# Seven block products for eight in the up projections of three feed-forward nets of a decoder trunk, on one Trainium2 core

## The chip, the core and the metric

The kernel runs on one core of a Trainium2 chip. The metric is the time on the device in microseconds (us), as the median of several runs. Before the change three runs gave 2679.24, 2676.48 and 2678.54 us, so the median is **2678.54 us**.

The engines are named as the profile names them: PE is the tensor engine (matmuls), PEld its weight loads, DVE the vector engine, ACT the scalar engine, POOL is GpSimd, SP is the engine that issues most transfers (DMA).

## What is computed

One step of a decoder trunk with two layers, for 544 tokens in all: 512 of a prompt and 32 of samples (8 sequences of 4 tokens). The model width is 1024. Each layer is a feed-forward net (ffn1), a mixing half (attention beside a convolution) and a second feed-forward net (ffn2), with a layer norm behind each:

```
def swiglu(x, w_up, w_down):                    # w_up 1024 x 5632, w_down 2816 x 1024
    a, u = jnp.split(x @ w_up, 2, axis=-1)
    return (jax.nn.silu(a) * u) @ w_down

x = layer_norm(ALPHA * x + 0.5 * swiglu(x, p['ffn1_up'], p['ffn1_down']), p['ln1_g'], p['ln1_b'])
q, k, v, glu, gates = jnp.split(x @ p['w_in'] + p['b_in'], SPLITS, axis=-1)
...
x = layer_norm(ALPHA * x + mix @ p['w_out'], p['ln2_g'], p['ln2_b'])
x = layer_norm(ALPHA * x + 0.5 * swiglu(x, p['ffn2_up'], p['ffn2_down']), p['ln3_g'], p['ln3_b'])
```

All tensors are float32. There are four feed-forward nets in the program: ffn1 and ffn2 of layer 0, ffn1 and ffn2 of layer 1, in this order, each pair with a mixing half between.

## The kernel before

Features lie on the 128 partitions, tokens on the free axis. The activations X are four tiles (`pr` in the profile), each with two chunks of 128 features x 544 tokens. The tokens are worked in two parts, cut at 280: `hf` 0 has 280 columns, `hf` 1 has 264.

**Halves of a number.** PE works on the type fp32r. To keep float32 accuracy each operand is held as two tiles, a high one (a cast on ACT: L251 for weights, L301 for activations) and the rest (a subtraction on DVE: L254, L302). A product takes three matmuls: `wh` by h, `wh` by lo, `wl` by h (L292 to L294, in `unit`). A unit is 256 output columns (two of 128, `m`) for one token part: with 8 chunks `k` of the inner dimension it has 8 x 2 x 3 = 48 matmuls, into one PSUM tile `pa`.

**A feed-forward net** (`ffn`, L410) has 11 column blocks j of 256 columns, in groups of 3, 3, 3 and 2. For a block, `up` (L432) makes two units of the gate weights (key "a"), each followed by a SiLU on ACT (L418), then two units of the other weights ("u"), each followed by the product on DVE (L424) and a split into halves (L301, L302). `up_first` (L441) does blocks 0 and 1, all of token part 0 ahead of part 1, because the norm before it delivers X in two parts. After the first block of a group, the down products of the group before are made (`down`, L458) and added into the residual tiles Y on DVE (L456). Block 10 and the last group end the net, with the layer norm (`tail`, `ln_fin`). `residual` (L400) makes the start of Y, ALPHA times X, from the two halves of X: a multiplication on ACT and L405 on DVE.

**Weights.** `plan` lists all pieces of weights in the order of use. `fetch` loads the next piece (256 columns x 8 chunks, 1 MB) by a DMA on SP (L162) into a tile `raw` of a pool of its own (`wp`, three buffers of 8 KB per partition). `prep` splits it by two casts of 1024 elements per partition on ACT and two subtractions on DVE into `wh` and `wl`, which are tiles of the large pool `pp` (36 buffers of 4 KB, called "pair", shared with X, Y, H and the tiles of attention). `W` hands out the next piece, and first calls `prep` until LA pieces (2; LAU 3 and LAV 2 in the up projections) are under way. Pool `fp` (6 buffers, tiles `f`) holds small activations. PSUM has three tiles of two banks (`ps2`, named `pa`) and two of one bank (`ps1`, named `pb`).

**What sets the order.** The program is written once in Python; a scheduler of the tile framework then puts each engine's instructions in one order, and each engine runs them strictly in that order. An instruction waits for the tiles that it reads, and for the buffer that it writes to be released.

**The mixing half** (`mix`, L716) makes keys, values, queries, gates and a gated input of a convolution by units of the same kind; the first weights are "k" and "ug", whose unit is followed by sigmoids on ACT (L771). The taps of the convolution (L806) run on DVE.

Of the kernel before, what the change touches and what calls it, by code (L numbers as in the profile page):

```python
# [25 lines left out]
CUT = 280  # L26
# [27 lines left out]
LA, LAU, LAV, TAP, LAG, WPB, FPB = 2, 3, 2, 1.2, 0.0, 3, 6  # L54
# [6 lines left out]
TF = 0  # L61
PPB = 36
# [34 lines left out]
class Ker:  # L97
    def __init__(self, ctx, tc, a):
# [3 lines left out]
        self.wp = pool("wp", WPB)  # L102
# [52 lines left out]
    def plan(self):  # L155
# [74 lines left out]
    def fetch(self, cut=0):  # L230
        """the load of the next piece of weights, in cut parts"""
        key, kk, load = self.pieces[self.loaded]
        self.loaded += 1
        raw = self.wp.tile([128, 8, 256], F32, tag="raw", name=self.nm("raw"))
        n = kk // max(cut, 1)
        for k in range(0, kk, n):
            dma = load(raw[:, k:k + n], k) if cut > 1 else load(raw[:, :kk])
            if cut:
                self.tc.keep_in_program_order(dma)
        return key, kk, raw  # L240

    def prep(self, pin=False, got=None):
        nc = self.nc
        key, kk, raw = got or self.fetch()
        ms = []
        for k in range(0, kk, 4):
            n = min(4, kk - k)
            src = raw[:, k:k + n, :]
            wh = self.pp.tile([128, 4, 256], F32R, tag="pair", name=self.nm("wh"))
            wl = self.pp.tile([128, 4, 256], F32R, tag="pair", name=self.nm("wl"))  # L250
            ins = nc.scalar.copy(wh[:, :n], src)  # L251
            if pin:
                self.tc.keep_in_program_order(ins)
            ins = nc.vector.tensor_tensor(wl[:, :n], src, wh[:, :n].bitcast(F32), op=ALU.subtract)  # L254
# [10 lines left out]
    def ahead(self, n):  # L265
        """n pieces of weights, and no more, split before what follows"""
# [44 lines left out]
    def ln_fin(self, acc, Y, hf, emit):  # L311
        """the norm from the sums on, in two steps, each begun by products"""
# [49 lines left out]
    def rsqrt(self, src, n, w):  # L362
        """1 / sqrt(src + EPS) for a few columns: a seed from the bits, one step of Newton's, one of third order"""
# [20 lines left out]
    def ln_out(self, X, l, vg, vb, func=AF.Identity):  # L384
        vec = self.vec[l]

        def emit(p, y, hs):
            xf = self.f1([128, 2, hs.stop - hs.start])
            for m in range(2):
                c = 2 * p + m  # L390
                self.nc.scalar.activation(xf[:, m], y[:, m, hs], func,  # L391
                                          scale=vec[:, vg + c:vg + c + 1], bias=vec[:, vb + c:vb + c + 1])
            xh, xl = X[p]
            self.split(xh[:, :, hs], xl[:, :, hs], xf)
        return emit

# [832 lines left out]
```

## Time and profile before

| what | value |
|---|---|
| median of three runs | 2678.54 us |
| span of the profiled execution | 2676.0 us (the page gives no other time of this execution) |
| POOL busy | 282.4 us, 11% |
| L292, L293, L294 (the split products) | 6336 matmuls each, of 20638 on PE |
| largest idle times of PE by what ended them, by the groups of its lines | 11.5 us DVE L254, 6.7 us and 4.8 us DVE L302 |
| transfers | 232.14 MB, mean 87 GB/s |

The busy time of an engine is the time in which an instruction of it was under way; the share is of the span. Matmuls overlap, so the mean duration of one (about 0.29 us) is more than twice the distance between two (0.125 us). The lines of the page and of the trace on which the argument rests are shown where it is made.

### The profile page before, as it was taken

The page shows a single profiled execution, that of the slowest core. Times are in us where ns is not written, and L with a number is a line of the kernel's source. Part 1 is how long each engine was busy: PE and PEld are TensorE (multiplying, and loading weights), DVE is VectorE, ACT ScalarE, POOL GpSimd, SP SyncE. Part 2 cuts the span into 40 slices and gives each one's busy share as a digit, 9 for nine tenths or more (in the row PEclk, how much of TensorE's full clock was granted, in tenths as well). Part 3 has the DMA queues.
Part 4 walks back from the last instruction along what each step waited for, and adds up shares of the span by engine and source line. Part 5 has one row for each costly group of instructions (what it writes and reads, how often), then busy time and mean ns, then how long its engine had stood idle before and what let it go on. Part 6 is the DMA issues. An engine that isn't in the chain of part 4 may idle for free.

```text
span 2676.0 us, 47289 instructions
## 1 busy us (share of the span) xinstructions
PE 2610.9 (98%) x20638; PEld 2561.6 (96%) x20638; DVE 1430.8 (53%) x2135; ACT 978.6 (37%) x1646; POOL 282.4 (11%) x532
## 2 busy tenths in 40 slices
PE   8999999999999999999999999999999999999997
PEld 7999999989899999999999999999899999999997
DVE  4323246897976554243453233469989665433235
ACT  4222125577426342222242222246863352422211
POOL 2000001532300000000110000025141000000001
PEclk9999999999999999999999999999999999999998
DMA  7223133222322233132332222233223222222221
GB/s 222 82 83 107 48 111 83 59 86 66 83 86 80 73 99 107 64 102 73 110 111 95 79 91 76 72 83 87 69 63 103 79 94 80 80 91 86 80 84 42
DMA packets 250089, 232.14 MB, mean 87 GB/s; under 512 B 40433, under 2 KB 247485, under 8 KB 249785
## 3 DMA queue, kind: packets, MB, share of 16 engines
q1 hardware_dynamic: 246073, 220.35, 26.7%
q0 software_dynamic: 3808, 8.76, 1.1%
q8 instruction: 162, 2.65, 0.4%
q14 instruction: 46, 0.38, 0.0%
HBM read 225.69 MB, written 9.16 MB: 88 GB/s over the span
## 4 chain that ended last, share of the span: by engine, by line
PE 86%; DVE 5%; POOL 3%; ACT 2%; issue 1%; DMA 1%; SPq 0%; DVEq 0%; POOLq 0%; ACTq 0%
PE pa L292 27%; PE pa L294 27%; PE pa L293 27%; DVE pr L806 2%; POOL f L821 2%; DVE wl L254 1%; PE pa L916 1%; PE pb L945 1%; PE pb L957 1%; DMA raw<-in_ffn_up_dram 1%; DVE pr L302 1%; POOL nw L372 0%; PE pb L353 0%; ACT wh L251 0%; PE pa L1039 0%
## 5 line engine op out<-in xcount | busy, mean ns | idle before, releaser
L292 PE MATMUL pa<-pr,wh 128*128 128x264 f32 (+2 forms) x6336 | 1838.7, 291 | 19.2 <-DVE pr L302 4.8
L293 PE MATMUL pa<-pr,wh 128*128 128x264 f32 (+2 forms) x6336 | 1831.8, 289 | 6.7 <-DVE pr L302 6.7
L294 PE MATMUL pa<-pr,wl 128*128 128x264 f32 (+2 forms) x6336 | 1825.7, 289 | 11.5 <-DVE wl L254 11.5
L292 PEld LDWEIGHTS pa<-pr,wh 128*128 128x128 f32 x6336 | 1193.2, 189 | 27.5 <-ACT pr L301 5.8
L294 PEld LDWEIGHTS pa<-pr,wl 128*128 128x128 f32 x6336 | 1196.2, 189 | 13.7 <-DVE wl L254 12.8
L293 PEld LDWEIGHTS pa<-pr,wh 128*128 128x128 f32 x6336 | 1195.9, 189 | 10.8 <-DVE pr L302 8.8
L254 DVE TENSOR_TENSOR wl<-raw,wh 128x1024 fp32r<-128x1024 f32 (+1 forms) x424 | 483.0, 1165 | 191.0 <-ACT wh L251 190.5
L251 ACT CAST wh<-raw 128x1024 fp32r<-128x1024 f32 (+1 forms) x424 | 406.3, 999 | 403.7 <-PE pa L293 324.5
L424 DVE TENSOR_TENSOR f<-pa,f 128x560 f32<-128x560 f32 (+2 forms) x88 | 63.6, 722 | 536.2 <-PE pa L294 496.9
L806 DVE SCALAR_TENSOR_TENSOR pr<-u,cw,pr 128x512 f32<-128x512 f32 x480 | 344.9, 768 | 1.7 <-ACT pr L799 1.7
L301 ACT CAST pr<-f 128x560 fp32r<-128x560 f32 (+1 forms) x162 | 102.4, 646 | 356.7 <-DVE f L424 302.1
L418 ACT ACTIVATE f<-pa 128x560 f32<-128x560 f32 (+2 forms) x88 | 54.9, 624 | 428.4 <-PE pa L294 428.1
L371 POOL TENSOR_SCALAR nw<-nw 94x3 f32<-94x3 f32 (+3 forms) x16 | 7.0, 436 | 1712.1 <-DVE nw L367 1712.1
L456 DVE SCALAR_TENSOR_TENSOR pr<-pa,pr 128x560 f32<-128x560 f32 (+3 forms) x128 | 92.3, 722 | 165.8 <-PE pa L294 165.4
L302 DVE TENSOR_TENSOR pr<-f,pr 128x560 fp32r<-128x560 f32 (+1 forms) x162 | 115.6, 723 | 55.0 <-ACT pr L301 53.8
L821 POOL TENSOR_TENSOR f<-f,cw 128x124 f32<-128x124 f32 x128 | 103.6, 847 | 1.6 <-ACT f L760 1.4
L391 ACT ACTIVATE f<-pr,vec 128x280 f32<-128x280 f32 (+1 forms) x80 | 42.6, 604 | 82.0 <-DVE pr L357 82.0
L930 ACT ACTIVATE at<-at,sm 128x257 f32<-128x257 f32 (+1 forms) x128 | 60.5, 476 | 12.8 <-DVE sm L926 12.5
L357 DVE TENSOR_TENSOR pr<-pr,pb 128x560 f32<-128x560 f32 (+1 forms) x56 | 36.6, 716 | 48.9 <-PE pb L353 48.9
L332 ACT ACTIVATE pr<-pr 128x560 f32<-128x560 f32 (+1 forms) x14 | 9.2, 657 | 132.6 <-DVE pr L328 132.6
L926 DVE CUSTOM_DVE_ANT_0 at<-pa,nd,nsk 128x256 f32<-128x256 f32 (+1 forms) x128 | 50.3, 445 | 11.1 <-PE pa L916 11.1
L934 ACT ACTIVATE at<-at,sm 128x256 f32<-128x256 f32 (+1 forms) x128 | 50.9, 473 | 4.3 <-DVE sm L932 4.2
(181 smaller groups left out, 1243.0 us busy)
## 6 DMA issues: line engine op xcount, KB each, us to landing
raw<-in_ffn_up_dram SPq DMA_DIRECT2D x87, 1024.0 KB, 5.3
raw<-in_ffn_down_dram SPq DMA_DIRECT2D x48, 768.0 KB, 4.5
raw<-in_w_in_dram SPq DMA_DIRECT2D x36, 1024.0 KB, 5.2
raw<-in_ffn_down_dram SPq DMA_DIRECT2D x16, 512.0 KB, 3.5
raw<-in_w_in_dram SPq DMA_DIRECT2D x32, 256.0 KB, 5.0
raw<-in_w_attn_out_dram SPq DMA_DIRECT2D x32, 256.0 KB, 4.6
raw<-in_w_conv_out_dram SPq DMA_DIRECT2D x8, 1024.0 KB, 5.1
raw<-in_w_out_dram SPq DMA_DIRECT2D x8, 1024.0 KB, 5.0
```

The source lines that it names most:

```text
L251: ins = nc.scalar.copy(wh[:, :n], src)
L254: ins = nc.vector.tensor_tensor(wl[:, :n], src, wh[:, :n].bitcast(F32), op=ALU.subtract)
L292: self.nc.tensor.matmul(o, lhsT=wh, rhs=h, start=k == 0, stop=False)
L293: self.nc.tensor.matmul(o, lhsT=wh, rhs=lo, start=False, stop=False)
L294: self.nc.tensor.matmul(o, lhsT=wl, rhs=h, start=False, stop=k == kk - 1)
L301: pin(self.nc.scalar.copy(hi, src))
L302: pin(self.nc.vector.tensor_tensor(lo, src, hi.bitcast(F32), op=ALU.subtract))
L424: nc.vector.tensor_tensor(sa, ps, sa, op=ALU.mult)
L456: nc.vector.scalar_tensor_tensor(Y[p][:, :, hs], ps, 0.5, Y[p][:, :, hs], op0=ALU.mult, op1=ALU.add)
L806: self.last["cw"] = nc.vector.scalar_tensor_tensor(cc[:, m, 0:SEQ], u[:, m, k:k + SEQ], cw[:, 8 * k + c:8 * k + c + 1], cc[:, m, 0:SEQ], o ...
L821: nc.gpsimd.tensor_tensor(pr[:, 4 * b:4 * b + 4, :], win, wv.unsqueeze(1).to_broadcast([128, DS, KC]), op=ALU.mult)
L930: nc.scalar.activation(P[:, c, :nk + 1], P[:, c, :nk + 1], AF.Exp, scale=-1.0, bias=negm[:, c:c + 1], accum_out=den[:, c:c + 1])
```

## The change

The token cut moves from 280 to 272, so that both token parts are equal. In three of the four nets (not ffn1 of layer 0), blocks j = 2 to 9 go through a new function, `up_fast`. It takes a "piece" of 128 gate columns and 128 columns of the other weights (two pieces for a block). Inner dimension and tokens are cut in two each: the even and the odd chunks of 128 of each tile of X, and the two token parts. The 2 x 2 blocks of the weights (A11, A12 of the gate, A21, A22 of the other) are multiplied with the 2 x 2 blocks of X by Strassen's scheme in Winograd's form, with 7 block products where the plain way has 8:

- `combine` makes the sums of weight blocks on DVE (L290 to L293, 512 elements per partition each; L291 writes in place) and splits them and the blocks themselves into halves (L265 on ACT, L266 on DVE). Its tiles are `raw`, `ls` and an `f`.
- `right` makes the sums of X blocks once for each tile of X, from the norm's float32 output, when its second token part is there (L450 to L452 on DVE, then a split). They are kept in tiles T for the whole net. For this the norm's output is written into Y in place (L435).
- `product` is one block product: 4 chunks x 3 matmuls of 272 columns into one PSUM bank. A block product is added to what the bank has, or opens it.
- Between products, ACT copies a bank into another bank (L564) or into an `f` tile (L566, L569), DVE adds two of the results (L571, L575), and ACT makes two SiLUs (L573, L551). `finish` makes product 3 of a piece after product 7 of the next piece, and then L551, L552 (the product on DVE) and the split (L346, L347).
- The residual of these nets is Y itself, scaled in place on ACT (`scaled`, L470), where it was made from the halves of X before.

The other lines follow from these: weights are loaded in tiles of half the size, in the pool `pp`, which has 39 buffers now; the pool `wp` is gone; `fp` has 10 buffers; the look-ahead of fast pieces is LAS = 2. In line numbers of the changed kernel the units' matmuls are L337 to L339, those of block products L537, the splits of weights L265 and L266, those of activations L346 and L347, and L424 has become L489.

```
-CUT = 280
+CUT = 272
-LA, LAU, LAV, TAP, LAG, WPB, FPB = 2, 3, 2, 1.2, 0.0, 3, 6
+LA, LAU, LAV, LAS, TAP, LAG, FPB = 2, 3, 2, 2, 1.2, 0.0, 10
-PPB = 36
+PPB = 39
+FAST = range(2, 10)
-        self.wp = pool("wp", WPB)
...
+        def fast(key, w, j):
+            def load(dst, r):
+                c0 = (DFF if r else 0) + j * 128
+                return self.nc.sync.dma_start(dst, w[:, c0:c0 + 128].rearrange("(k p) c -> p k c", p=128))
+            out.append((key, 0, load))
...
+    def combine(self, La, Lu):
+        v = self.nc.vector
+        Ls = self.pp.tile([128, 2, 4, 128], F32, tag="pair", name=self.nm("ls"))
+        L4 = self.f1([128, 4, 128])
+        blk = lambda t, m: t.rearrange("p (q m) c -> p m q c", m=2)[:, m]
+        a11, a12, a21, a22 = blk(La, 0), blk(La, 1), blk(Lu, 0), blk(Lu, 1)
+        s3, s2 = Ls[:, 0], Ls[:, 1]
+        v.tensor_tensor(s3, a11, a21, op=ALU.subtract)
+        v.tensor_tensor(a21, a21, a22, op=ALU.add)
+        v.tensor_tensor(s2, a21, a11, op=ALU.subtract)
+        v.tensor_tensor(L4, a12, s2, op=ALU.subtract)
+        a = self.halves(La, [128, 8, 128])[0]
+        s = self.halves(Ls, [128, 2, 4, 128])[0]
+        u = self.halves(Lu, [128, 8, 128])[0]
+        f = self.halves(L4, [128, 4, 128], True)[0]
...
+    def right(self, y):
+        v = self.nc.vector
+        t = self.pair()
+        th, tl = self.hl()
+        t4 = t.rearrange("p m (h n) -> p (m h) n", h=2)
+        b = y.rearrange("p m (h n) -> p m h n", h=2)
+        v.tensor_tensor(t4[:, 0:2], b[:, :, 1], b[:, 0], op=ALU.subtract)
+        v.tensor_tensor(t4[:, 2], b[:, 1, 1], t4[:, 0], op=ALU.subtract)
+        v.tensor_tensor(t4[:, 3], b[:, 1, 0], t4[:, 2], op=ALU.subtract)
+        self.split(th, tl, t)
...
+        def product(i, o, w, start=False):
+            wh, wl = w[i]
+            for q in range(4):
...
+                mm(wh[:, q], h, start and q == 0)
+                mm(wh[:, q], lo)
+                mm(wl[:, q], h, last=q == 3)
...
+        def finish():
+            s = st.pop("s", None)
+            if s is None:
+                return
+            product(3, s["A"], s["w"])
+            sa, pu, (hh, hl), m = s["sa"], s["pu"], s["h"], s["m"]
+            nc.scalar.activation(sa[:, 1], s["A"], AF.Silu)
+            nc.vector.tensor_tensor(sa, sa, pu, op=ALU.mult)
+            self.split(hh[:, m]..., hl[:, m]..., sa)
+
+        def up_fast(g, j, h, m):
+            w = self.W(l, f, "s", 2 * j + m, la=LAS)[0]
+            ps = self.p2()
+            b1, E = ps[:, 0, :CUT], ps[:, 1, :CUT]
+            A = self.p1()[:, :CUT]
+            nc.tensor.matmul(A, lhsT=w[1][0][:, 0], rhs=X[0][0][:, 0, :CUT], start=True, stop=True, skip_group_check=True)
+            pu, sa = self.act(0), self.act(0)
+            product(1, b1, w, True)
+            nc.scalar.copy(A, b1)
+            product(7, E, w, True)
+            nc.scalar.copy(pu[:, 1], E)
+            finish()
+            product(6, A, w)
+            nc.scalar.copy(pu[:, 0], A)
+            product(4, E, w)
+            nc.vector.tensor_tensor(pu[:, 0], E, pu[:, 0], op=ALU.add)
+            product(2, b1, w)
+            self.last["up"] = nc.scalar.activation(sa[:, 0], b1, AF.Silu)
+            product(5, A, w)
+            nc.vector.tensor_tensor(pu[:, 1], A, pu[:, 1], op=ALU.add)
+            st["s"] = {"A": A, "w": w, "sa": sa, "pu": pu, "h": h, "m": m}
```

The number of matmuls in the program goes from 20350 to 19822: 3 x 6336 in `unit` become 3 x 4800, and 4032 of `product` and 48 of the line that opens the bank (L561) come in.

**The vector queue where the fast blocks begin.** The next rows are DVE's order in ffn2 of layer 0 before, from the splits of the weights of block 3 (`wl`; those of block 2 stand earlier) to the first product of block 2 (the last row). The rows with `f982` and `f985` belong to the last two units of `up_first` that end with a product.

```order
L254 TENSOR_TENSOR wl1003_10321<-raw1001_10318,wh1002_10320 128x1024
L254 TENSOR_TENSOR wl1005_10325<-raw1001_10318,wh1004_10324 128x1024
L302 TENSOR_TENSOR pr958_9803<-f982_10129,pr957_9802 128x2x264
L254 TENSOR_TENSOR wl1012_10433<-raw1010_10430,wh1011_10432 128x1024
L254 TENSOR_TENSOR wl1014_10437<-raw1010_10430,wh1013_10436 128x1024
L424 TENSOR_TENSOR f985_10232<-pa986_10234,f985_10232 128x528
L302 TENSOR_TENSOR pr960_9805<-f985_10232,pr959_9804 128x2x264
L424 TENSOR_TENSOR f1007_10377<-pa1017_10442,f1007_10377 128x560
```

Now the same place reads as follows; L489 is what L424 was, for the last unit of `up_first`, and the rows from L290 on make the weights of the first fast piece.

```order
L489 TENSOR_TENSOR f1053_10398<-pa1054_10400,f1053_10398 128x544
L290 TENSOR_TENSOR ls1059_10462<-raw1057_10458,raw1058_10460 128x512
L291 TENSOR_TENSOR raw1058_10460<-raw1058_10460 128x4x128
L266 TENSOR_TENSOR wl1062_10469<-raw1057_10458,wh1061_10468 128x1024
L292 TENSOR_TENSOR ls1059_10462<-raw1058_10460,raw1057_10458 128x512
L347 TENSOR_TENSOR pr1020_9943<-f1053_10398,pr1019_9942 128x2x272
L293 TENSOR_TENSOR f1060_10463<-raw1057_10458,ls1059_10462 128x512
L266 TENSOR_TENSOR wl1064_10473<-ls1059_10462,wh1063_10472 128x1024
L266 TENSOR_TENSOR wl1066_10477<-raw1058_10460,wh1065_10476 128x1024
L266 TENSOR_TENSOR f1068_10481<-f1060_10463,f1067_10480 128x512
```

Before, the splits of the next weights stood ahead of the product of the last unit of `up_first` (L424 with `f985`); now the sums and splits of the first fast piece stand behind it.

**The scalar queue in the steady stretch of fast pieces.** Before, in ffn2 of layer 0, ACT's order at a block is two SiLUs, a cast of the gated product, and the casts of the weights to come:

```order
L418 ACTIVATE f1089_11405<-pa1088_11356 128x560
L418 ACTIVATE f1091_11456<-pa1090_11407 128x528
L301 CAST pr1097_11468<-f1089_11405 128x2x280
L251 CAST wh1102_11576<-raw1101_11574 128x1024
L251 CAST wh1104_11580<-raw1101_11574 128x512
L251 CAST wh1111_11688<-raw1110_11686 128x1024
```

Now, in ffn1 of layer 1, there are two kinds of pieces. L551 is the second SiLU of a piece, after its product 3; L566 copies E (`pa`) of the next piece out, which product 4 of that piece then adds into. The first kind:

```order
L551 ACTIVATE f1694_15693<-pb1692_15690 128x272
L265 CAST wh1703_15804<-ls1699_15794 128x1024
L265 CAST f1707_15812<-f1700_15795 128x512
L265 CAST wh1705_15808<-raw1698_15792 128x1024
L346 CAST pr1661_15536<-f1694_15693 128x544
L566 COPY f1711_15819<-pa1709_15816 128x272
```

And the second kind, one piece later:

```order
L551 ACTIVATE f1712_15820<-pb1710_15817 128x272
L265 CAST f1723_15937<-f1716_15920 128x512
L265 CAST wh1721_15933<-raw1714_15917 128x1024
L566 COPY f1727_15944<-pa1725_15941 128x272
L569 COPY f1727_15944<-pb1726_15942 128x272
L346 CAST pr1695_15788<-f1712_15820 128x544
```

Where ACT had only casts for later use behind a SiLU, a copy that PE's next products wait for now stands behind three casts and L346, or behind two casts. PE's order in this stretch is product 1 of the next piece and L561, products 4 and 5 of a piece, product 7 of the next, products 2 and 3, product 6 of the next; between the end of product 3 and the first matmul of product 4 stand 21 matmuls in the first kind, 25 in the second.

**The scalar queue where the mixing half begins.** Before, in layer 0, the casts of the second weights in use ("ua", `wh390` and `wh392`) and of the next pieces stand right behind the last cast of the keys (L301) and ahead of the first sigmoids (L771):

```order
L301 CAST pr366_4144<-f388_4228 128x2x280
L251 CAST wh390_4238<-raw389_4236 128x1024
L251 CAST wh392_4242<-raw389_4236 128x1024
L251 CAST wh407_4351<-raw406_4349 128x1024
L251 CAST wh409_4355<-raw406_4349 128x1024
L251 CAST wh413_4415<-raw412_4410 128x1024
```

Now they stand behind the sigmoids (L899 is what L771 was; "ua" is `wh423` and `wh425`):

```order
L346 CAST pr398_4210<-f420_4294 128x2x272
L899 ACT_TABLE_LOAD
L899 ACTIVATE f434_4410<-pa427_4314,vec067_712 128x272 x2
L265 CAST wh423_4306<-raw421_4302 128x1024
L265 CAST wh425_4310<-raw422_4304 128x1024
L265 CAST wh437_4417<-raw435_4413 128x1024
L265 CAST wh439_4421<-raw436_4415 128x1024
```

The casts of "ua" are now behind two activations that wait for the first unit of "ug".

More of the change, by code (lines that the diff above doesn't have):

```diff
@@ L233, in fetch @@
         self.loaded += 1
[L234 to L239, printed above, removed]
-        return key, kk, raw
+        raw = []
+        for k in range(0, kk or 8, 4):
+            n = min(4, (kk or 8) - k)
+            t = self.pp.tile([128, n, 256] if kk else [128, 8, 128], F32, tag="pair", name=self.nm("raw"))
+            if cut > 1:
+                for d in range(0, n, cut):
+                    self.tc.keep_in_program_order(load(t[:, d:d + cut], k + d))
+            else:
+                dma = load(t, k)
+                if cut:
+                    self.tc.keep_in_program_order(dma)
+            raw.append(t)
@@ L242, in prep, with halves @@
+        return key, kk, raw
+    def halves(self, t, shape, small=False):
+        new = lambda n: (self.f1(shape, F32R) if small else
+                         self.pp.tile(shape, F32R, tag="pair", name=self.nm(n)))
+        wh, wl = new("wh"), new("wl")
+        ins = self.nc.scalar.copy(wh, t)
+        self.nc.vector.tensor_tensor(wl, t, wh.bitcast(F32), op=ALU.subtract)
+        return (wh, wl), ins
     def prep(self, pin=False, got=None):
-        nc = self.nc
         key, kk, raw = got or self.fetch()
+        if not kk:
+            self.ready.append((key, self.combine(*raw), kk))
+            return
@@ L245, in prep @@
         ms = []
[L246 to L251, printed above, removed]
+        for t in raw:
+            m, ins = self.halves(t, list(t.shape))
             if pin:
                 self.tc.keep_in_program_order(ins)
-            ins = nc.vector.tensor_tensor(wl[:, :n], src, wh[:, :n].bitcast(F32), op=ALU.subtract)
-            ms.append((wh, wl))
+            ms.append(m)
@@ L382, in rsqrt, with ln_out @@
         return r
-    def ln_out(self, X, l, vg, vb, func=AF.Identity):
+    def ln_out(self, X, l, vg, vb, T=None, func=AF.Identity):
         vec = self.vec[l]
         def emit(p, y, hs):
-            xf = self.f1([128, 2, hs.stop - hs.start])
             for m in range(2):
                 c = 2 * p + m
-                self.nc.scalar.activation(xf[:, m], y[:, m, hs], func,
+                self.nc.scalar.activation(y[:, m, hs], y[:, m, hs], func,
                                           scale=vec[:, vg + c:vg + c + 1], bias=vec[:, vb + c:vb + c + 1])
             xh, xl = X[p]
-            self.split(xh[:, :, hs], xl[:, :, hs], xf)
-        return emit
+            self.split(xh[:, :, hs], xl[:, :, hs], y[:, :, hs])
+            if T is not None and hs.stop == NT:
+                T.append(self.right(y))
+        return emit
+    def right(self, y):
[8 more added lines that the diff above has]
+        self.split(th, tl, t)
+        return [x.rearrange("p m (h n) -> p (m h) n", h=2) for x in (th, tl)]
     def hl(self):
@@ L407, in residual, with scaled, ffn @@
         return Y
-    def ffn(self, l, f, X, vg, vb, last):
+    def scaled(self, Y):
+        for y in Y:
+            self.nc.scalar.mul(y, y, ALPHA)
+        return Y
+    def ffn(self, l, f, XYT, vg, vb, last):
         nc = self.nc
+        X, Y0, T = XYT
         H = {}
@@ L433, in up @@
             j = 3 * g + i
+            if self.is_fast(l, f, j):
+                h = new_h(g)
+                for m in range(2):
+                    up_fast(g, j, h, m)
+                return
+            finish()
             w = self.W(l, f, "a", j, la=LAU if j < 9 else LAV)
```

60 lines of the change are left out of this document (43 added, 17 removed).

## The prediction

> **What bounds the kernel now.** I read the page first (busy shares, clock, the chain that ended last), then the busy time by stretches, then the groups of instructions by shape.
>
> ```profile
> PE 2610.9 (98%) x20638; PEld 2561.6 (96%) x20638; DVE 1430.8 (53%) x2135; ACT 978.6 (37%) x1646; POOL 282.4 (11%) x532
> PE 86%; DVE 5%; POOL 3%; ACT 2%; issue 1%; DMA 1%; SPq 0%; DVEq 0%; POOLq 0%; ACTq 0%
> 991.00:1308.00 317.00, 317.00 (x2524) 317.00 (x2523) 102.24 (x118) 71.57 (x90) 0.00 (x0) 1.00 0.27 86
> 1396.00:1714.00 318.00, 318.00 (x2530) 317.82 (x2529) 104.33 (x122) 75.03 (x94) 0.00 (x0) 1.00 0.27 87
> 2270.00:2632.00 362.00, 359.77 (x2853) 359.13 (x2852) 125.57 (x147) 93.56 (x120) 3.33 (x13) 1.00 0.25 80
> 1427.00:1475.00 48.00, 48.00 (x384) 48.00 (x384) 17.61 (x20) 11.25 (x13) 0.00 (x0) 1.00 0.29 91
> ```
>
> TensorE is busy for 98% of the span and holds 86% of the chain. The next three rows are the feed-forward stretches that the change touches (columns: stretch, length, then PE, weight load, DVE, ACT, POOL busy, clock, DMA). PE has no gap there, at full clock, while DVE is busy for a third of the time and ACT for a quarter. The last row gives the pace: 384 matmuls in 48.00 us, **0.125 us each**, as a mean of 280 and 264 columns; the new 272 is that mean. A matmul less in these stretches is 0.125 us less, as long as DVE and ACT keep up.
>
> **The change, part by part.** *Removed matmuls.* A column block costs 2 weights x 2 halves x 8 x 2 x 3 = 192 matmuls now. Afterwards it is two pieces of 7 products x 4 x 3 = 84, and one extra matmul each (L561) that opens the bank: 170. 22 fewer x 8 blocks x 3 nets = 528, x 0.125 = **-66.0 us**. Per piece, PE needs 85 x 0.125 = 10.6 us, against 12.0 now.
>
> *Vector and scalar work per piece.* The rows (by shape, then from the timeline):
>
> ```profile
> L254 DVE TENSOR_TENSOR wl<-raw,wh 128x1024 fp32r<-128x1024 f32 x376 | 455.1, 1227 | 191.0 <-ACT wh L251 190.5 <-PE pa L294 0.2
> L254 DVE TENSOR_TENSOR wl<-raw,wh 128x512 fp32r<-128x512 f32 x48 | 32.9, 686 | 0.0
> L302 DVE TENSOR_TENSOR pr<-f,pr 128x560 fp32r<-128x560 f32 x81 | 59.5, 741 | 33.7 <-ACT pr L301 33.5
> L782 DVE SCALAR_TENSOR_TENSOR u<-pa,vec,f 128x280 f32<-128x280 f32 x16 | 7.4, 502 | 1.0 <-ACT f L771 1.0
> L806 DVE SCALAR_TENSOR_TENSOR pr<-u,cw,pr 128x512 f32<-128x512 f32 x480 | 344.9, 768 | 1.7 <-ACT pr L799 1.7
> L251 ACT CAST wh<-raw 128x1024 fp32r<-128x1024 f32 x376 | 382.5, 1048 | 386.8 <-PE pa L293 307.6 <-DMA raw<-in_ffn_up_dram 31.7 <-DMA raw<-in_w_in_dram 15.9
> L251 ACT CAST wh<-raw 128x512 fp32r<-128x512 f32 x48 | 29.5, 615 | 16.9 <-PE pa L293 16.9
> L301 ACT CAST pr<-f 128x560 fp32r<-128x560 f32 x81 | 52.4, 658 | 260.5 <-DVE f L424 224.2 <-DVE f L1179 36.2
> L1082 ACT ACTIVATE f<-pa,vec 128x280 f32<-128x280 f32 x16 | 7.0, 492 | 26.4 <-PE pa L294 26.4
> L959 ACT COPY pr<-pb 128x256 f32<-128x256 f32 x32 | 11.8, 368 | 9.5 <-PE pb L957 9.2
> ```
>
> DVE: four block sums of 512 (0.69 each, by the 512 split), three splits of 1024 (1.23) and one of 512 (0.69), two sums out of PSUM (0.50), a product and a split of 544 (0.74): 9.6 us. ACT: 3 x 1.05 + 0.62, five of 272 out of PSUM (0.49), one cast of 0.66: 6.9 us. Both lie under PE's 10.6, DVE with little to spare. The block sums might take 0.69 to 0.77 (L806, also f32 of 512); the copy that writes PSUM (L564) is not in the trace: 0.37 to 0.66 by the last two rows above, taken at 0.49.
>
> ```profile
> 940.41 2.94 ACT L251 CAST wh<-raw 128x1024 fp32r<-128x1024 f32 x3
> 690.47 0.88 ACT L1082 ACTIVATE f<-pa,vec 128x280 f32<-128x280 f32 x2 [0.26 <-PE pa L294]
> 1485.50 0.29 PE L294 MATMUL pa<-pr,wl 128*128 128x280 f32 x1
> 1485.83 0.64 ACT L418 ACTIVATE f<-pa 128x560 f32<-128x560 f32 x1 [6.71 <-PE pa L294]
> 1497.56 0.29 PE L294 MATMUL pa<-pr,wl 128*128 128x280 f32 x1
> 1497.95 0.74 DVE L424 TENSOR_TENSOR f<-pa,f 128x560 f32<-128x560 f32 x1 [16.95 <-issue]
> 962.55 2.59 DVE L302 TENSOR_TENSOR pr<-f,pr 128x528 fp32r<-128x528 f32 x4
> ```
>
> Back to back, each starts a little before the last one ends: three casts in 2.94 are 0.95 apart, two activations 0.39. Of the next two rows, the last matmul starts at 1485.50, its 0.13 slot ends at 1485.63, and ACT starts 0.20 later; by the two after them DVE starts 0.26 later. The last row has four operations of 528 in 2.59, which is 0.64 apart; sums of 512 are then about 0.6 apart, and the cast of 544 (L346) about 0.57.
>
> *Steady pieces.* By the order, ACT copies E (L566) behind the SiLU of the piece before (L551) and some casts; the matmuls of product 4 wait for that copy, because they add into E. In the first of the two ACT pieces shown above, L551, 1024, 512, 1024, L346, L566 stand in a row: 0.20 + 0.39 + 0.95 + 0.52 + 0.95 + 0.57 + 0.49 = 4.1 us from the end of product 3. PE's order has 21 matmuls in between, 2.6 us: it waits **1.5 us**. In the second (L551, 512, 1024, L566) it is 2.6 against 25 matmuls, 3.1 us: no wait. The two alternate; the first stands at 4 pieces of each net: 12 x 1.5 = **+18 us** (0 to 30).
>
> *The start of the fast pieces.* As the DVE rows show, the first block sum stands behind L489, which needs the end of the last ordinary unit. From that end: 0.26, L489 0.64, L290 0.6, L291 0.6, split 1.23: the third matmul of product 1 is 3.0 us late (two matmuls and L561 fill 0.4). Products 7 and the next piece's 1 wait for their own splits in the same queue, 1.3 and 1.4. That is 5.7, taken as 6; in layer 1's first net the first cast stands behind one more ACT cast, and the second piece's behind three: 8. Sum **+20 us** (6 to 30).
>
> ```profile
> PE pa L294 <- DVE wl L254: 3.6, 1, 3.6
> 700.00:703.00 3.00, 0.00 (x0) 0.00 (x0) 3.00 (x4) 1.65 (x2) 0.00 (x0) 0.50 0.00 0
> 706.00:709.00 3.00, 3.00 (x15) 3.00 (x14) 3.00 (x4) 0.00 (x0) 0.00 (x0) 0.50 0.97 336
> ```
>
> One thing can make these dearer: after a wait of 3.6 us near 700, PE ran at clock 0.50 and did 15 matmuls in 3 us, where 24 are normal. My 3.0 us lies below that wait, so I add nothing; if it happens at all three it is about 2 us each, inside the bounds. [...]
>
> *Moved and pooled.* Raw weights lose their own pool (three of 8 KB) and share the pair pool, now 39 instead of 36. A DMA starts when a pair tile is released. In steady pieces the order puts that 86 matmuls (10.8 us) ahead of use.
>
> ```profile
> raw<-in_ffn_up_dram SPq DMA_DIRECT2D x87, 1024.0 KB, 5.3
> raw<-in_ffn_down_dram SPq DMA_DIRECT2D x16, 512.0 KB, 3.5
> ```
>
> A 512 KB load with rows of half the length is in no row: 3.5 to 5.3 us, taken at 5.3; with sum, sum and split (2.6) it needs 8, under 10.8. At the start of each mixing half, the cast of the second weight now stands behind the two sigmoids of the first unit; 0.20 + 0.8 + 1.05 + 1.2, less what PE has, is 2.6 us, twice: **+5** (0 to 8). Other pieces stand closer to their use than before (some 20 to 30 matmuls, where 50 was usual): an estimate of **+5** (0 to 15). If SP waits for a release, all loads behind it wait too.
>
> *Residual and right-hand blocks.* Building T adds, per pair, 544 + 272 + 272 + a split of 1088 on DVE, four times: about 11.5 us; the residual's four go.
>
> ```profile
> 965.06 4.90 DVE L405 SCALAR_TENSOR_TENSOR pr<-pr,pr 128x1088 f32<-128x1088 f32 x4
> ```
>
> By the order nearly all of T stands behind the last split of X, and T is needed only after four more units of 48 matmuls (24 us): 0. Without that cover it would be up to 6.6 us per net.
>
> Sum: -66 + 18 + 20 + 5 + 5 = **-18 us**. The profiled execution's span is 2676.0; its own time isn't given apart, and the three runs shown have a median of 2678.54, 2.5 above. 2678.5 - 18 gives **2660**.
>
> **The rivals.**
>
> *All of it arrives.* DVE and ACT have 1.0 and 3.7 us of slack per piece, and ACT waits may dissolve if PE's shift moves L551 early. Against it: the rows stand in a fixed order, and the handover is 4.1 against 2.6. Then -66 + 6 + 5: 2623. Chance 0.15.
>
> *It cancels.* The waits reach 66 us: every piece waits about 0.8 us more than summed. 2673 to 2684. Chance 0.13.
>
> *It gets slower: the vector queue becomes the bound in steady pieces.* Place: the loop L575, L290, L291, split, L292, cast on ACT, L551, casts, L566, product 4. It decides when the loop passes 11.5 us per piece, since (66 - 30) / 40 pieces = 0.9 us above 10.6. At 12.0 it would be 40 x 1.4 = 56, and -66 + 56 + 20 + 10 = +20: 2699. For it: DVE is at 9.6 of 10.6, and the loop has four handovers. Against it: back-to-back rows overlap, which leaves DVE at about 8.7. Chance 0.17.
>
> *It doesn't do what it says.* Twelve matmuls in a row go into one bank now, where three went before; the trace has no such run. If they took 0.132 us, 4032 x 0.007 = 28 us more: 2688. Chance 0.05.
>
> **How the numbers follow.** My forecast, 2645 to 2672, holds 0.50. The range 2622 to 2692 takes in most of the full gain, the cancelling and the lower part of slower, and leaves out about 0.2. Faster by over 0.2% (what a measurement of this kernel can tell from no change) means under 2673: 0.50 + 0.15 and a little of the cancelling, 0.66; within 0.2%: 0.14; slower: 0.20.
>
> **What would show it.** PE should count about 20110 matmuls, 0.125 us apart inside products. Right: PE waiting for ACT's L566 by some 1.5 us at every other piece; three clusters of PE waits on DVE's splits, of 5 to 9 us, at the first fast piece of each net; DVE at 80% to 90% there. Wrong: PE full in these stretches (then 2623), waits at every piece, waits for DMA, or a wider spacing of matmuls. Gaps in the mixing halves above today's would mean the shared pool costs more than I gave it.

## The result, and the profile after

The changed kernel takes 2699.53 us (median of 4 runs, 2699.02 to 2702.08), beside 2677.51 us for the kernel before in the same runs: a ratio of **1.0089, 95% interval 1.0074 to 1.0103**. It is slower by 0.9%; the forecast was 2660, with a range up to 2692. The profiled execution has a span of 2697.8 us, 21.8 more than before.

From the page of the changed kernel, the busy times and the chain that ended last:

```profile
PE 2568.8 (95%) x20110; PEld 2515.7 (93%) x20110; DVE 1695.7 (63%) x2555; ACT 1115.0 (41%) x1946; POOL 269.7 (10%) x532
PE 78%; DVE 9%; ACT 6%; DMA 3%; POOL 2%; issue 2%; SPq 0%; DVEq 0%; POOLq 0%; ACTq 0%
```

PE has the 528 matmuls less. Its time without work (span less busy) went from 65.1 to 129.0 us, **64 us more**. Its busy time fell by 42.1, where 528 x 0.125 = 66 were removed; the other 24 go with a slower clock (0.988 before, 0.975 now, as the mean of the execution). So -66 + 64 + 24 = +22, which is the difference of the spans. From the answers by stretches, a fast stretch of layer 0's second net and its steady part, and then (from the chain that ended last) 24 matmuls of block products in the net after it, layer 1's first:

```profile
1000.00:1310.00 310.00, 297.52 (x2317) 294.98 (x2316) 187.58 (x248) 118.35 (x192) 0.00 (x0) 0.98 0.32 95
1097.00:1142.00 45.00, 42.94 (x341) 42.50 (x340) 35.73 (x49) 22.40 (x41) 0.00 (x0) 1.00 0.25 71
```

```profile
1510.85 3.03 PE pa L537 x24
```

PE, full in this stretch before, now lacks 12.5 of 310 us. In the steady part PE works for 42.94 of 45 us and DVE is busy for 35.73 of 45 us (79%), ACT for half. A block product's matmuls are 0.126 us apart, as those of units are (0.125: in PE's timeline an L337 starts at 999.73 and the 18th matmul behind it at 1001.98).

**Where the time went.** Each norm starts with the same pair of matmuls (L323, now L368), so these mark the stages. In the timeline, the marks at both ends of layer 0's mixing half, before and then after:

```profile
405.48 0.63 PE L323 MATMUL pb<-pr,ones 128*128 128x280 f32 x2
908.58 0.64 PE L323 MATMUL pb<-pr,ones 128*128 128x280 f32 x2
```

```profile
404.51 0.62 PE L368 MATMUL pb<-pr,ones 128*128 128x272 f32 x2
930.25 0.62 PE L368 MATMUL pb<-pr,ones 128*128 128x272 f32 x2
```

| stage | before | after | difference |
|---|---|---|---|
| first net of layer 0 (no block products) | 405.5 | 404.5 | -1.0 |
| mixing half, layer 0 | 503.1 | 525.7 | **+22.6** |
| second net, layer 0 | 406.4 | 399.6 | -6.8 |
| first net, layer 1 | 410.9 | 407.2 | -3.7 |
| mixing half, layer 1 | 503.3 | 520.9 | **+17.6** |
| second net, layer 1, to the end | 446.8 | 439.9 | -7.0 |

The nets that were changed give 17.5 us. The two mixing halves, in which no block product is made, take 40.2 us more. A small part of this is where the marks lie: in each mixing half some 20 matmuls (2.5 us) that stood behind its closing mark before stand ahead of it now. Without that shift the halves take some 35 us more, and the nets give some 12.

The waits of PE in the timeline of the changed kernel, three in layer 0's mixing half and then four in the fast net behind it:

```profile
576.64 0.59 PE L337 MATMUL pa<-pr,wh 128*128 128x272 f32 x1 [6.56 <-DVE sm L1054]
622.91 0.48 PE L1150 MATMUL pa<-ident,at 128*128 128x128 f32 x1 [4.62 <-ACT at L1142]
721.85 0.60 PE L339 MATMUL pa<-pr,wl 128*128 128x272 f32 x1 [5.88 <-DVE wl L266]
...
1005.79 0.59 PE L537 MATMUL pa<-pr,wl 128*128 128x272 f32 x1 [2.90 <-DVE wl L266]
1017.60 0.51 PE L537 MATMUL pa<-pr,wh 128*128 128x272 f32 x2 [1.90 <-ACT f L566]
...
1122.70 0.52 PE L537 MATMUL pa<-pr,wh 128*128 128x272 f32 x2 [1.08 <-ACT f L566]
1145.37 0.52 PE L537 MATMUL pa<-pr,wh 128*128 128x272 f32 x2 [1.08 <-ACT f L566]
```

The first two have no counterpart before; the third was 3.6. The first is at attention: L1054 is the softmax's operation on DVE. What stands ahead of it there, in DVE's timeline, before (L806 are taps of the convolution, L926 the softmax) and after (L934 and L1054):

```profile
557.69 0.67 DVE L824 TENSOR_REDUCE pr<-f 128x16 f32<-128x496 f32 x1 [0.43 <-POOL f L821]
558.27 2.13 DVE L806 SCALAR_TENSOR_TENSOR pr<-u,cw,pr 128x512 f32<-128x512 f32 x3
560.33 1.22 DVE L254 TENSOR_TENSOR wl<-raw,wh 128x1024 fp32r<-128x1024 f32 x1
561.46 0.74 DVE L806 SCALAR_TENSOR_TENSOR pr<-u,cw,pr 128x512 f32<-128x512 f32 x1
562.13 1.21 DVE L254 TENSOR_TENSOR wl<-raw,wh 128x1024 fp32r<-128x1024 f32 x1
...
564.58 0.47 DVE L926 CUSTOM_DVE_ANT_0 at<-pa,nd,nsk 128x256 f32<-128x256 f32 x1
```

```profile
563.37 0.67 DVE L952 TENSOR_REDUCE pr<-f 128x16 f32<-128x496 f32 x1 [0.42 <-POOL f L949]
563.96 5.45 DVE L934 SCALAR_TENSOR_TENSOR pr<-u,cw,pr 128x512 f32<-128x512 f32 x8
569.33 1.22 DVE L266 TENSOR_TENSOR wl<-raw,wh 128x1024 fp32r<-128x1024 f32 x1
570.47 2.07 DVE L934 SCALAR_TENSOR_TENSOR pr<-u,cw,pr 128x512 f32<-128x512 f32 x3
572.46 1.22 DVE L266 TENSOR_TENSOR wl<-raw,wh 128x1024 fp32r<-128x1024 f32 x1
...
574.89 0.48 DVE L1054 CUSTOM_DVE_ANT_0 at<-pa,nd,nsk 128x256 f32<-128x256 f32 x1
```

The softmax comes 6.9 us after the reduction starts before, and 11.5 after. Between them stand the same two splits of weights, but 12 taps in place of 5 (the rows left out are one tap and one split of activations in each): the splits, and what follows them, were put later into the queue. Taps are not urgent; the softmax is, since PE waits for it. What the shared pool changed is in SP's waits for the loads of weights (line, what it waited for, us in total, times, longest), before and then after:

```profile
SPq L162 <- DVE wl L254: 2003.7, 186, 41.3
```

```profile
SPq L162 <- PE pa L339: 658.3, 100, 29.2
SPq L162 <- DVE wl L266: 246.3, 57, 15.1
```

Before, a load waits for the split that frees a raw buffer. Now most wait for a matmul, which fits a buffer of the shared pool that is freed by the last use of split weights, and that is later. In the fast nets a late load holds PE up as the kernel runs. The chain behind a wait for L566 in layer 1's first net begins with a load that SP can issue only when a split has freed a buffer (rows of the chain, with the sums, splits and casts between them left out):

```profile
1495.59 5.30 DMA raw<-in_ffn_up_dram
1500.98 0.69 DVE ls L290
...
1507.57 1.77 PE pa L537 x12
```

At the softmax it does not. If loads and casts are matched in their order, the weights of the two splits had landed at 507.1 before, with the first of their casts at 556.5, and at 546.7 after, with that cast at 565.3. They came closer to their use, but still 19 us ahead of it. So there the sharing can act only through the order that the scheduler chose.

**Theory A** is that this sharing costs the 40 us. **Rival B** is the equal cut of the tokens, which shifts the blocks of the mixing half. **Rival C** is the block products themselves (their sums, splits and tiles).

### The profile page after: what moved, and what is told of

Read it like the earlier page. It is cut to its first block, busy times and chain, and to the rows that moved or that the text cites. A ratio compares the mean times of both kernels' runs of the same rounds, so it can differ in the third digit from the quotient of the medians.

```text
span 2697.8 us, 47547 instructions
## 1 busy us (share of the span) xinstructions
PE 2568.8 (95%) x20110; PEld 2515.7 (93%) x20110; DVE 1695.7 (63%) x2555; ACT 1115.0 (41%) x1946; POOL 269.7 (10%) x532
## 4 chain that ended last, share of the span: by engine, by line
PE 78%; DVE 9%; ACT 6%; DMA 3%; POOL 2%; issue 2%; SPq 0%; DVEq 0%; POOLq 0%; ACTq 0%
PE pa L337 20%; PE pa L339 20%; PE pa L338 19%; PE pa L537 8%; PE pb L537 6%; DMA raw<-in_ffn_up_dram 3%; DVE pr L934 3%; DVE wl L266 2%; POOL f L949 2%; ACT wh L265 2%; ACT pr L346 1%; PE pa L1044 1%; DVE pr L347 1%; PE pb L1073 1%; DVE raw L291 0%
## 5 line engine op out<-in xcount | busy, mean ns | idle before, releaser
L337 PE MATMUL pa<-pr,wh 128*128 128x272 f32 (+2 forms) x4800 | 1402.0, 293 | 31.7 <-DVE sm L1054 13.1
L339 PE MATMUL pa<-pr,wl 128*128 128x272 f32 (+2 forms) x4800 | 1397.1, 292 | 19.0 <-DVE wl L266 19.0
L338 PE MATMUL pa<-pr,wh 128*128 128x272 f32 (+2 forms) x4800 | 1392.4, 290 | 5.9 <-DVE pr L347 5.9
L337 PEld LDWEIGHTS pa<-pr,wh 128*128 128x128 f32 x4800 | 912.3, 190 | 39.1 <-DVE sm L1054 14.0
L339 PEld LDWEIGHTS pa<-pr,wl 128*128 128x128 f32 x4800 | 912.5, 190 | 23.1 <-DVE wl L266 21.2
L338 PEld LDWEIGHTS pa<-pr,wh 128*128 128x128 f32 x4800 | 919.1, 191 | 8.7 <-DVE pr L347 7.5
L265 ACT CAST wh<-raw 128x1024 fp32r<-128x1024 f32 (+1 forms) x424 | 413.1, 999 | 379.7 <-DMA raw<-in_ffn_up_dram 109.1
L266 DVE TENSOR_TENSOR wl<-raw,wh 128x1024 fp32r<-128x1024 f32 (+1 forms) x424 | 488.8, 1164 | 114.5 <-ACT wh L265 69.6
L934 DVE SCALAR_TENSOR_TENSOR pr<-u,cw,pr 128x512 f32<-128x512 f32 x480 | 343.9, 771 | 2.2 <-ACT pr L927 2.2
L537 PE MATMUL pa<-pr,wh 128*128 128x272 f32 x1536 | 304.5, 295 | 29.2 <-ACT f L566 21.5
L537 PEld LDWEIGHTS pa<-pr,wh 128*128 128x128 f32 x1536 | 245.6, 192 | 35.7 <-ACT f L566 25.7
L537 PE MATMUL pa<-pr,wl 128*128 128x272 f32 x768 | 225.2, 293 | 7.3 <-DVE wl L266 7.3
L581 DVE SCALAR_TENSOR_TENSOR pr<-pa,pr 128x544 f32<-128x544 f32 (+2 forms) x128 | 92.1, 722 | 182.0 <-PE pa L339 181.8
L346 ACT CAST pr<-f 128x544 fp32r<-128x544 f32 (+1 forms) x122 | 78.5, 648 | 202.9 <-DVE f L489 134.0
L537 PEld LDWEIGHTS pa<-pr,wl 128*128 128x128 f32 x768 | 147.8, 192 | 8.4 <-DVE wl L266 8.4
L537 PE MATMUL pb<-pr,wh 128*128 128x272 f32 x768 | 153.9, 292 | 0.0
L489 DVE TENSOR_TENSOR f<-pa,f 128x544 f32<-128x544 f32 (+2 forms) x40 | 28.9, 722 | 170.3 <-PE pa L339 156.3
L537 PEld LDWEIGHTS pb<-pr,wh 128*128 128x128 f32 x768 | 123.7, 192 | 0.0
L537 PE MATMUL pb<-pr,wl 128*128 128x272 f32 x384 | 111.5, 292 | 0.0
L347 DVE TENSOR_TENSOR pr<-f,pr 128x544 fp32r<-128x544 f32 (+1 forms) x122 | 87.6, 720 | 24.4 <-ACT pr L346 23.9
```

What stands on the lines that cost most here:

```text
L265: ins = self.nc.scalar.copy(wh, t)
L266: self.nc.vector.tensor_tensor(wl, t, wh.bitcast(F32), op=ALU.subtract)
L337: self.nc.tensor.matmul(o, lhsT=wh, rhs=h, start=k == 0, stop=False)
L338: self.nc.tensor.matmul(o, lhsT=wh, rhs=lo, start=False, stop=False)
L339: self.nc.tensor.matmul(o, lhsT=wl, rhs=h, start=False, stop=k == kk - 1)
L346: pin(self.nc.scalar.copy(hi, src))
```

## The experiments

All times of a table row are compared with runs of the kernel before on the same chip, whose medians lay between 2671.5 and 2673.2 us.

| run | us | ratio to before | 95% interval |
|---|---|---|---|
| e1, cut alone | 2682.58 | 1.0042 | 1.0029 to 1.0054 |
| e2, all but the products | 2714.94 | 1.0154 | 1.0139 to 1.0169 |
| e3, own pool | 2653.48 | 0.9926 | 0.9911 to 0.9941 |
| e4, copy first | 2699.16 | 1.0096 | 1.0081 to 1.0111 |
| e5, own pool, no products | 2700.41 | 1.0104 | 1.0086 to 1.0122 |
| e6, own pool of five | 2660.37 | 0.9951 | 0.9933 to 0.9969 |
| e7, e6 and sink copies on DVE | 2654.41 | 0.9930 | 0.9914 to 0.9947 |
| e8, e3 and sink copies on DVE | 2636.59 | 0.9870 | 0.9846 to 0.9893 |
| e9, changed, look-ahead 3 | 2675.84 | 1.0009 | 0.9997 to 1.0020 |
| e10, before, look-ahead 3 | 2646.59 | 0.9894 | 0.9874 to 0.9913 |
| e11, e8, look-ahead 3 | 2635.91 | 0.9855 | 0.9830 to 0.9880 |

**e1: the cut alone**, in the kernel before.

```
-CUT = 280
+CUT = 272
```

> The kernel before with the token cut at 272 alone. The two mixing halves cost 40 us more after the change. Theory A (the weights that share the pool of the pair tiles set another order there): the cut does nothing, 2673 to 2683 us. Rival B (the equal halves shift the mixing half): 2710 to 2720 us. Rival C (the block products' own tiles, sums and splits disturb it): 2673 to 2683 us, like A.

Its mixing halves take 502.5 and 502.9 us by the marks, as before. Rival B, which needed 40 us there, is out. The runs are 0.4% slower all the same, with a wide spread (2677 to 2686 us), while the profiled one, at 2677.05, has a span of 2675.3; no wait in its trace says where up to 10 us would be. That stays open.

**e2: all but the products**, in the changed kernel.

```
-FAST = range(2, 10)
+FAST = ()
-                Y += self.scaled(Y0) if Y0 else self.residual(X)
+                Y += self.residual(X)
-        T = [] if fast else None
+        T = None
```

> The changed kernel with no block product at all: all up projections by ordinary units, no sums of X blocks, the residual from the halves of X; the shared pool, the half-size loads, the equal cut and the norm in place remain. Theory A (shared pool): the mixing halves stay as slow as in the changed kernel and the feed-forward nets go back to their times before, 2710 to 2722 us. Rival B (cut): the same. Rival C (block products disturb the mixing halves): 2673 to 2683 us.

Rival C is out: the mixing halves take 524.4 and 528.5 us without any block product. The waits in its timeline are those of the changed kernel:

```profile
574.08 0.59 PE L337 MATMUL pa<-pr,wh 128*128 128x272 f32 x1 [6.57 <-DVE sm L1054]
620.51 0.33 PE L1150 MATMUL pa<-ident,at 128*128 128x128 f32 x1 [4.60 <-ACT at L1142]
```

**e3: a pool of their own for the raw weights**, in the changed kernel; the number of 4 KB buffers in both pools together stays 39. (Two lines are added, so its line numbers are the changed kernel's plus 2.)

```
-PPB = 39
+PPB = 35
+WPB = 4
+        self.wp = pool("wp", WPB)
-            t = self.pp.tile([128, n, 256] if kk else [128, 8, 128], F32, tag="pair", name=self.nm("raw"))
+            t = self.wp.tile([128, n, 256] if kk else [128, 8, 128], F32, tag="raw", name=self.nm("raw"))
```

> The changed kernel with a pool of its own for the raw weights: four buffers of 4 KB, taken from the pair pool (35 for 39). Theory A: the mixing halves are as fast as before the change, so 40 us less than changed, and some waits for the copy of E (L566) go as well, because its row stands better on ACT: 2640 to 2662 us. Rivals B and C: no gain, 2690 to 2705 us; fewer pair tiles could also make the fast pieces wait for transfers, then above 2705 us.

With the same memory the time falls by 46 us (by the medians) and is 0.7% below the kernel before. Loads wait for splits again, the waits of 6.56 and 4.62 us at attention are gone, and so are all the waits for the copy of E (L566, here L568) in the steady pieces. From its SP waits, its steady part of layer 0's second net, and DVE's rows ahead of the same softmax (here L1056; L936 are the taps):

```profile
SPq L164 <- DVE wl L268: 1372.7, 254, 38.8
1097.00:1142.00 45.00, 45.00 (x361) 45.00 (x360) 30.41 (x43) 21.73 (x39) 0.00 (x0) 1.00 0.30 92
```

```profile
568.97 2.80 DVE L936 SCALAR_TENSOR_TENSOR pr<-u,cw,pr 128x512 f32<-128x512 f32 x4
...
572.83 1.41 DVE L936 SCALAR_TENSOR_TENSOR pr<-u,cw,pr 128x512 f32<-128x512 f32 x2
...
575.92 0.48 DVE L1056 CUSTOM_DVE_ANT_0 at<-pa,nd,nsk 128x256 f32<-128x256 f32 x1
```

PE is full in the steady part. Ahead of the softmax stand 6 taps where the changed kernel has 12, and it comes 7.5 us after the reduction (568.38) in place of 11.5. So theory A holds for these places, but not for all of the 40 us: by the marks, 26 of the 46 us come from the three changed nets (1246.7 to 1220.8 us) and 20 from the mixing halves (1046.6 to 1026.3); without the shift of the marks, which e3 does not have, these are 31 and 15. From PE's and then ACT's timeline:

```profile
526.29 0.47 PE L1075 MATMUL pb<-ident,at 128*128 128x128 f32 x1 [9.24 <-ACT at L1064]
```

```profile
522.75 0.41 ACT L1060 ACTIVATE at<-at,sm 128x129 f32<-128x129 f32 x1 [9.86 <-POOL at L1053]
```

Its mixing halves are still 513.0 and 513.3 us, 10 above before each: a new wait (9.24 and 8.48 us) stands at the first block of attention in each layer. The exponentials wait for a small copy of the sinks on POOL (L1053), which stands there behind stores of keys and values that POOL issues. Whether this comes from the pool of four or from something else that the change brought (half-size loads, more `f` tiles, the norm in place) no run separates; e5, without block products, has the same 20 us.

**e4: the copy of E ahead of the SiLU**, in the changed kernel.

```
-            nc.scalar.activation(sa[:, 1], s["A"], AF.Silu)
+            self.tc.keep_in_program_order(nc.scalar.activation(sa[:, 1], s["A"], AF.Silu))
-            nc.scalar.copy(pu[:, 1], E)
+            self.tc.keep_in_program_order(nc.scalar.copy(pu[:, 1], E))
```

> The changed kernel with the copy of E (L566) and the second SiLU (L551) held in the order in which the program has them, so that the copy stands ahead of that SiLU on ACT. If the 18 waits of about 1.1 us at L566 are the order of the ACT queue, they go, with the slower clock behind them: 2675 to 2682 us. Rival: the next weights' splits are late instead, and less than 5 us is gained: 2695 to 2700 us.

The rival holds. ACT's timeline of e4:

```profile
1125.58 1.05 ACT L265 CAST wh<-ls 128x1024 fp32r<-128x1024 f32 x1 [0.20 <-DVE ls L292]
1126.54 0.61 ACT L265 CAST f<-f 128x512 fp32r<-128x512 f32 x1
1127.05 1.05 ACT L265 CAST wh<-raw 128x1024 fp32r<-128x1024 f32 x1
1128.00 0.37 ACT L566 COPY f<-pa 128x272 f32<-128x272 f32 x1
```

The copy is ahead of L551 now, but behind three casts of weights, the first of which waits for a block sum. PE's waits for L566 are even 1.6 us here. What holds the copy is the late weights, not the SiLU; in e3, where the loads come in time, the waits are gone.

**e5: own pool without products** (the edits of e2 and e3 together).

> e3 (own pool for the raw weights) without any block product: ordinary units, no sums of X blocks, the residual from the halves of X. What e3 gains against this is the worth of the block products where the loads come in time. Theory A: the three nets of e3 have kept some 14 us each of the 22 us of matmuls, so this takes 2653.5 + 43 = 2697 us, of which the mixing halves are still 20 us above the kernel before. Rival: the own pool of four with 35 pair tiles is good for ordinary units too, and this is at 2673 to 2680 us, so that the products bring only 20 to 27 us.

The block products bring 1.0104 - 0.9926 = 1.8% (48 us) with loads in time, and 1.0154 - 1.0089 = 0.65% (17 us) with the shared pool. So the sharing costs the fast pieces some 30 us beside what it costs the mixing halves; the nets of the changed kernel and of e3 say the same (26 us by the marks, 31 without their shift).

**e6: five own buffers**, 34 pair tiles. **e7: in e6, the sink copies on DVE. e8: in e3, the same.**

```
-PPB = 35
-WPB = 4
+PPB = 34
+WPB = 5
...
-            nc.gpsimd.tensor_copy(P[:, :, nk].rearrange("p (r t) -> p r t", r=2), sinks)
+            nc.vector.tensor_copy(P[:, :, nk].rearrange("p (r t) -> p r t", r=2), sinks)
```

> e3 with five own buffers and 34 pair tiles. The stores of the values stand ahead of those of the keys on POOL here, so that the 9 us waits for a POOL copy (L1053) at the start of attention, that e3 shows in both layers, should be gone or shorter, with the slow clock behind them: 2630 to 2645 us. Rival: with 34 pair tiles the fast pieces wait for buffers: 2653 to 2670 us.

> e6 with the copies of the sinks into the softmax tile on DVE in place of POOL, so that no store issued on POOL stands ahead of them. If that queue holds back attention, both waits of 9 us go: 2630 to 2640 us, some 10 us below e6 if e6 still has them, or within 5 us of e6 if it has not.

> e3 (four own buffers, 35 pair tiles) with the copies of the sinks on DVE as in e7. e7 had mixing halves 5 us shorter in sum each than e6, but the feed-forward nets of five buffers and 34 pair tiles; e3's nets are 2 to 5 us shorter each. If both add up: 2638 to 2647 us, faster than all others. Rival: DVE, with 4 more copies at each softmax, gives it back elsewhere: 2650 to 2656 us, like e3.

e6 missed its forecast: it still has waits of 8.66 and 7.88 us that go back to the copy on POOL (L1053), and its three fast nets are 2 to 5 us longer each than e3's. In e7 both 9 us waits are gone and the mixing halves fall from 514.0 and 509.1 to 507.1 and 508.8; 4 and 6 us go back in their second parts, behind the convolution's norm. e8 adds e7's copy to e3's pools: mixing halves of 504.7 and 502.8, as before the change, and 2636.59 us, 1.3% faster than before. As the copy is an edit of its own, this shows where the other 20 us stood, not that the sharing had put them there.

**e9: look-ahead 3**, in the changed kernel with its shared pool; **e10: the same in the kernel before; e11: in e8.**

```
-LA, LAU, LAV, LAS, TAP, LAG, FPB = 2, 3, 2, 2, 1.2, 0.0, 10
+LA, LAU, LAV, LAS, TAP, LAG, FPB = 3, 3, 2, 2, 1.2, 0.0, 10
```

> The changed kernel with a look-ahead of three pieces for two in the mixing halves and the down products; the pool stays shared. Theory A: the loads are late because the pair tile that they write is only released by matmuls, however early they are asked for, so the waits of the mixing halves stay, 2692 to 2706 us. Rival: the loads are asked for too late, and one piece more of look-ahead brings most of the 40 us back: 2660 to 2680 us.

> The kernel before with the same look-ahead of three, its raw weights in their own pool. e9 had gained 24 us, though its waits at attention stayed. If that gain was only the repair of what the shared pool did, the kernel before has nothing to gain, 2670 to 2678 us. If the later waits of the mixing half (3.6 and 1.8 us in each layer before) are a matter of look-ahead whatever the pool, it gains some 8 to 15 us: 2658 to 2666 us.

> e8 (own pool of four, sink copies on DVE) with the look-ahead of three. If the pool and the look-ahead mend different waits, the 4.7 and 3.4 us waits that e8 still has in each layer go too: 2615 to 2628 us. If they mend the same ones: 2634 to 2642 us.

e9 came out where the rival had put it, 24 us faster, which spoke against theory A. But its timeline keeps the two waits that the change had brought at attention:

```profile
574.84 0.60 PE L337 MATMUL pa<-pr,wh 128*128 128x272 f32 x1 [6.25 <-DVE sm L1054]
620.41 0.33 PE L1150 MATMUL pa<-ident,at 128*128 128x128 f32 x1 [3.90 <-ACT at L1142]
```

What went are the waits in the later part of the mixing half (L266, 5.88 and 1.8; one of 3.0 us for ACT has come in), which the kernel before has too, at 3.6 and 1.8. e10 settles it: the kernel before gains 25 us from the same edit, more than was expected. By the ratios, the change costs 0.9% with a look-ahead of two and 1.15% with three (1.0009 less 0.9894), so the look-ahead is a gain of its own and no repair. It doesn't add to e8: in e11 the waits of 4.7 and 3.4 us that e8 has in each layer are gone, as expected, but others come at attention (5.02 and 7.85 us for L1144), for 2635.91 in place of 2636.59 us. So the time is where the second forecast of e11 had put it, and not for its reason. e8 and e11 are the fastest, at 0.9870 and 0.9855, with intervals that overlap each other's and, for e8, that of e10 (0.9894). e10 is the kernel before with one number changed: beside it, the block products with all their repairs (e11, on the same chip) bring 10.7 us.

## Why the prediction was wrong, step by step

- **Removed matmuls, -66: right.** 20110 are counted, 0.126 us apart in products of 12. The rival of a wider spacing is out.
- **Steady pieces, +18: right in size, partly by luck.** The trace has 18 waits at L566 of 0.8 to 1.4 us, 19.6 in sum. The order put them at 12 places of 1.5; they stand at 18, three in each run of six pieces where two were counted. I took the ACT queue as given, without a wait in it. The chain behind such a wait starts with a load, and in e3, with loads in time, there is none.
- **Start of the fast pieces, +20: right in size, and in cause for the first wait.** 5.3, 6.8 and 6.2 us in the three nets. The late split was put at 3.0 us and is 2.90 in two of them. What follows are waits for ACT's copies (L564, L566), where the prediction had the splits of the next products. In layer 1's first net a cast takes 2.44 us, and 2.8 are a wait for the preparation of a constant (L820), which the prediction didn't have.
- **Slower clock behind the starts, 0: wrong.** The step added nothing, since 3.0 us lies below the wait of 3.6 behind which it saw the clock at 0.50. That misread the profile before, in whose row 700 to 703 the clock is at 0.50 while PE still waits. The clock fell at 699.07, right behind a wait of 2.21 us (to 698.98) and ahead of the one of 3.58:

```profile
698.98 0.55 PE L292 MATMUL pa<-pr,wh 128*128 128x280 f32 x1 [2.21 <-ACT f L1082]
703.34 0.60 PE L294 MATMUL pa<-pr,wl 128*128 128x280 f32 x1 [3.58 <-DVE wl L254]
```

```profile
699.07:709.31 10.24, 6.66 (x27) 6.33 (x28) 10.24 (x13) 1.99 (x2) 0.00 (x0) 0.50 0.31 102
```

  In the changed kernel, the clock fell at 1005.21, within the wait of 2.90 us that ends at 1005.79. In stretches of 4 us (the column before the last two is the clock):

```profile
1004.00:1008.00 4.00, 2.21 (x10) 2.21 (x10) 4.00 (x6) 1.05 (x1) 0.00 (x0) 0.65 0.00 0
1008.00:1012.00 4.00, 3.54 (x16) 3.22 (x16) 2.91 (x4) 2.79 (x4) 0.00 (x0) 0.50 0.00 0
```

  Busy time x (1 - clock), summed over all such stretches, grew by 11 us in the three nets and by 13 in the mixing halves. That is most of why the nets gave 17 us (12 without the shift of the marks) and not 28.
- **Moved and pooled, +5 and +5: the second is the step that failed.** The first, the later cast of the second weight, came as forecast: 1.48 and 0.76 us in layer 0, 1.31 and 0.74 in layer 1. The second priced the pool by how far ahead of its use a load starts. In its place the two mixing halves took 40 us more: 27 are waits (the idle times of PE in the two halves' timeline, 50 after and 23 before), some 5 the shift of the marks, and the rest goes with the slower clock. The largest waits, 6.56 us in each layer, are at a place where the loads are in time and the order of DVE is another, with taps ahead of the softmax that PE waits for. No row of the prediction looked there, though it named gaps in the mixing halves as the sign that the pool was priced too low. e2 shows that the cost needs no block product; e3 shows that the sharing causes some 15 of the 35 us that are not the shift, and some 30 in the nets besides. That the scheduler filled DVE with taps because the splits came late in its plan is read from the order, not tried, and the cause of the other 20 us stays open.
- **T and the residual, 0: right, as far as PE's waits show.** T of layer 0's second net is built from 975.25 us on, and PE has no wait from there to the first fast piece at 1005.79; it is the same in the other two nets.
- **The rivals.** "It gets slower" had the time (2699) and not the place: DVE is at 79% in steady pieces, a pair of pieces takes 22.7 us (1145.37 less 1122.70), 11.3 for one, below the 11.5 that it named, and the nets did get faster. In e3 DVE has 30.41 of 45 us and PE is full. The loss lay for the most part outside the loop that it priced. "All of it arrives" comes nearer in e5 and e3: 48 of 66 us once the loads come in time.

## What to carry to other kernels

A pool that is given away to make room for a change is part of the change: ask for each load which instruction frees the buffer that it will get, before and after, and look at SP's waits for it. When the order is a scheduler's, a change of pools can move work that it doesn't name; compare the queues of the changed kernel in the stages that the change doesn't name, at each place where the bounding engine waits for a short operation behind background work.

## What the runs showed of the hardware

In this case the clock of PE did not go by the length of a wait alone. The kernel before has the same wait of 1.82 us in both layers. In its timeline, and in the stretches that follow:

```profile
843.37 0.40 PE L294 MATMUL pa<-pr,wl 128*128 128x280 f32 x1 [1.82 <-DVE wl L254]
2162.41 0.40 PE L294 MATMUL pa<-pr,wl 128*128 128x280 f32 x1 [1.82 <-DVE wl L254]
```

```profile
844.00:848.00 4.00, 4.00 (x34) 4.00 (x33) 4.00 (x5) 3.20 (x4) 0.00 (x0) 1.00 0.40 126
2164.00:2168.00 4.00, 4.00 (x23) 4.00 (x23) 4.00 (x6) 2.29 (x3) 0.00 (x0) 0.65 0.70 234
```

The columns are those of the stretches above. After the first the clock stays at 1.00 and PE does 34 matmuls in 4 us; after the second it is 0.65, with 23. What else it went by, no run shows. Slow stretches also differ in length: beside the one of 10.24 us from 699.07 on, the kernel before has one of 6.83 and one of 3.41 us, in both of which PE is busy throughout at clock 0.50:

```profile
620.56:627.39 6.83, 6.83 (x37) 5.41 (x37) 0.91 (x1) 1.64 (x9) 0.19 (x1) 0.50 0.49 156
1333.95:1337.36 3.41, 3.41 (x15) 3.41 (x16) 2.01 (x4) 1.96 (x4) 0.00 (x0) 0.50 1.05 357
```

The wait of 3.6 us that the prediction went by is not the shortest that came with such a stretch: those of 2.21 us (to 698.98, clock 0.50 from 699.07 on) and 2.90 us (to 1005.79, clock 0.50 from 1005.21 to 1012.04) did as well.
